# A hybrid encoder layer: the output projection's weight sums made in another stage, and its first weight splits set one step behind their loads

## The chip, the cores and the metric

The kernel runs on one core of a Trainium2 chip. The metric is the device time of one execution in microseconds (us). Times are compared by the median of several runs.

## What is computed

One layer works on 2048 tokens of width 1024, in float32 throughout. Cut to what matters here, the reference is:

```python
u = rms_norm(h, g_mix_pre)
z = u @ w_in                                   # 1024 -> 2816 columns
qa, ka, va, qh, fh, ih, gh = split(z)
ya = swa_with_sinks(qa, ka, va, sinks)         # 8 heads of 64, window of 128 tokens
yh = hgrn2(qh, fh, ih, gh, lb, onorm)          # gated linear recurrence, 4 heads of 128, chunks of 64
y = concatenate([ya, yh]) @ w_out              # 1024 -> 1024, the "out projection"
h = h + rms_norm(y, g_mix_post)
h = h + rms_norm(cross_attention(rms_norm(h, g_x_pre), rms_norm(mem, g_mem), ...), g_x_post)
u = rms_norm(h, g_ffn_pre)
h = h + rms_norm((silu(u @ w_gate) * (u @ w_up)) @ w_down, g_ffn_post)
```

## The kernel before

**Products.** Every large product is made of float32 operands split in two parts, a rounded high part (ScalarE or GpSimd copies it) and the rest (VectorE subtracts it); three products of parts stand for one. Blocks of two token tiles or two column tiles go through a seven-product scheme (Strassen's, in Winograd's form): a block has seven steps of 12 matmuls of 128x512 (`seven`), and needs sums and differences of the quarters of both operands. The streamed operand's sums are made block by block (`streamed`, L1106). The other operand, of which four plain quarters and four sums are used by all blocks of a product, is called resident here (`resident`, tiles `T`). For weights, its sums are made once ahead and kept in a DRAM tensor: `sums` and `combined` load the quarters, add or subtract them on VectorE (L1034) and store the four results, in two halves each. That is eight VectorE operations, 20 loads and eight stores for `w_out`, whose tensor is `out_s`. `combined` is a generator: for each of the eight results it issues the loads, returns three times, and at the fourth call adds and stores.

**Stages.** `in_first` makes the input projection for the first 1024 tokens, with the seven-product scheme, from 0 to about 260 us. Eleven pairs of column blocks (`ORDER`) pass through it; four pairs hold a forget gate and its query (`fh`, `qh`), and after each of these comes `decays` (scan, exponentials, logarithm) on ScalarE, VectorE and GpSimd. `mix` then interleaves, up to about 630 us, three generators by hand: the rest of the input projection (`in_proj`, three products per split pair, no sums), the sliding-window attention (`swa`) and the recurrence (`hgrn`, one pair of chunks per call). Then, up to about 770 us, the last recurrence pairs run beside `fold_cross`, which multiplies the cross-attention's weights together. The remaining products (out projection, scores, values, feed-forward) follow in `phases`, out of pools of their own, to the end.

**Where the sums of w_out are made.** In `mix`, beside the second half of the attention: four calls of the generator `side` per attention pair. They use the tiles `u` (two buffers) and `x` (three), which the decays of `in_proj` use too.

**Where the first resident halves are made.** `phases` begins with a prologue for the out projection: eight halves of four `T` tiles. Each call loads one half into a tile `z` (two buffers, which hold the projected columns of `in_proj` too) and splits it at once. The loop over the last recurrence pairs calls it eight times, from the second pair on. All these loads are issued on SP's queue.

**Order.** Each engine and queue works in order. That order is not the order of the code alone: `TileContext(nc, schedule_with_timeline_sim=True)` lets a planner take, for each engine, the instruction that is ready first on a simulated timeline, with the order of the code as priority. `queued` and `behind` add edges that keep an instruction behind another one; `combined` uses `behind`, so that each sum stands behind the VectorE work of the step at which it is made. An instruction that fills a tile can be placed only once a buffer of that tile is free.

Of the kernel before, what the change touches and what calls it, by code (L numbers as in the profile page):

```python
# [11 lines left out]
F32 = mybir.dt.float32  # L12
# [6 lines left out]
P = 128  # L19
T = 2048  # L20
D = 1024
# [27 lines left out]
class Layer:  # L49
# [144 lines left out]
    def mix(self):  # L194
        tc, I = self.tc, self.I
        kw = dict(reuse_waits="tile")
        with contextlib.ExitStack() as left:
            def pool(name, at, **k):
                return at.enter_context(tc.tile_pool(name=name, bufs=1, **k, **kw))

            self.mc = pool("mc", left)
            self.r_x = self.cst.tile([P, NT], F32, name="r_x")
            with (
                tc.tile_pool(name="t1", bufs=3, **kw) as self.ts,
                tc.tile_pool(name="t2", bufs=3, **kw) as self.tb,
                tc.tile_pool(name="s1", bufs=2, side="right", **kw) as self.st_pool,
                contextlib.ExitStack() as at,
            ):
                self.banks(at, "ps1", **MOST)
                self.raws = 3  # L210
                u = self.in_first()
            self.banks(left, "ps2", **FOUR)
            self.hg = pool("hg", left)
            self.wp = pool("wp", left)
            self.io = pool("io", left)
            with tc.tile_pool(name="sw", bufs=1, side="right", **kw) as self.sw:
                self.zero_tiles()
                swa = self.swa(range(NT), lambda n: "st" if n < NPB else "sth")
                hgrn = self.hgrn(range(NPB), "h")
                cols = self.in_proj(1, u)  # L220
                next(cols)
                for _ in range(NPB + 1):
                    next(swa)
                    next(hgrn)
                    next(cols)
                for _ in hgrn:
                    pass
                self.out_sums, side = self.sums("out_s", self.w_out, 4, lambda: self.io_tile("u"), lambda: self.io_tile("x"))
                side = side()
                next(side)  # L230
                pairs = self.hgrn(range(NPB, NT), "gt")
                for i, _ in enumerate(swa, NPB + 2):
                    next(cols)
                    if i == NT + 1 - 0:
                        next(pairs)
                    for _ in range(4):
                        next(side, None)
                for _ in cols:
                    pass
            phases = self.phases(self.jobs(), None, lambda: self.io_tile("z"))  # L240
            with tc.tile_pool(name="xp", bufs=1, side="right", **kw) as self.xp:
                fold = self.fold_cross()
                for _ in range(2):
                    next(fold)
                for i, _ in enumerate(pairs, 1):
                    for _ in range(2):
                        next(fold)
                    if 2 <= i < 10:
                        next(phases)
                for _ in fold:  # L250
                    pass
            left.close()
            with (
                tc.tile_pool(name="t3", bufs=3, **kw) as self.ts,
                tc.tile_pool(name="t4", bufs=3, **kw) as self.tb,
                tc.tile_pool(name="s3", bufs=2, side="right", **kw) as self.st_pool,
                contextlib.ExitStack() as at,
            ):
                self.banks(at, "ps3", **MOST)
                self.raws = 4  # L260
                for _ in phases:
                    pass
# [188 lines left out]
    def in_first(self):  # L451
# [13 lines left out]
        T, raw = {}, {}  # L465
# [51 lines left out]
        def fetch():  # L517
            for s in range(2):
                for q in range(2):
# [9 lines left out]
        blocks = [("s",) + self.in_block(*p, tokens[i], tokens[i + 1], beside[i + 1], get if i > 9 else (), i < 2,  # L529
                                         None if i else lambda: x_loads(0, (2, 3)))  # L530
                  for i, p in enumerate(self.ORDER)]
# [1 line left out]
        plain = [b[1:4] + ([],) for b in blocks[:2]]  # L533
        blocks[:2] = ([(k, stream, out, lambda: iter(()), keep) for k, (stream, out, _, keep) in zip("qu", plain)]
                      + [("v", lambda kind: iter([None]), out, after, keep) for _, out, after, keep in plain])
        phases = self.phases([(lambda i, j, a, n: raw[i, j][:, a:a + n, :], 4, blocks, None, {})], T)
        PE, ACT, DVE, POOL = (getattr(mybir.EngineType, e) for e in ("PE", "Activation", "DVE", "Pool"))
        next(phases)
        self.turns("h", 36)
# [45 lines left out]
        u = []  # L585
# [633 lines left out]
    def phases(self, jobs, first, prologue=None):  # L1219
# [17 lines left out]
        T, keep = {}, [{} for _ in jobs]  # L1237
# [24 lines left out]
        def split(g):  # L1262

            if pending and pending[0][0] <= g:
                _, k, f = pending.pop(0)
                f()
                left[k] -= 1
                return True
            return False
# [54 lines left out]
                made[0] += 1  # L1324

        if not first:
            for i in range(8):
                half(-1, prologue)
                split(len(steps))
                yield  # L1330
        stream(0)
        yield
# [458 lines left out]
```

## Time and profile before

| | us |
|---|---|
| three timed runs, median (lowest to highest) | 2554.95 (2553.55 to 2556.43) |
| profiled execution, its own time | 2550.01 |
| span of the profiled execution, first to last instruction | 2548.3 |
| TensorE busy in it | 2504.8 |
| VectorE busy in it | 1792.1 |
| ScalarE busy in it | 1261.6 |
| mean granted TensorE clock | 0.997 |

The span is what the trace covers; the time of the profiled execution is 1.7 us longer, and the median of the timed runs 4.9 us longer still. In the profile's rows PE is TensorE, PEld its weight loads, DVE VectorE, ACT ScalarE, POOL GpSimd and SP the queue that issues the transfers. L990 and the like are lines of the kernel. A row of a timeline gives start, length, engine, line, operation, the tile written and those read, shape, count, and in brackets the idle time of the engine before it and what ended that. A row of stretches gives the stretch, its length, the busy time of PE, PEld, DVE, ACT and POOL, each with its number of instructions, the granted clock, the DMA share and GB/s.

### The profile page before, as it was taken

To read this page: it belongs to the slowest core of one execution; us is meant where nothing else is said; L and a number is where in the kernel's file an instruction comes from. 1 tells how busy PE (TensorE), PEld (TensorE's weight loads), DVE (VectorE), ACT (ScalarE), POOL (GpSimd) and SP (SyncE) were. 2 spreads that over 40 slices of the span, in tenths; PEclk is the share of its full clock that TensorE was granted. 3 is DMA by queue.
4 is the path that set the end of the run, shared out by engine and by line. 5 is a ranking of instruction groups with operands and counts; after the bars stand their busy time and mean duration, and the time that the engine had idled before them with its cause. 6 is when DMAs were issued, how large, how long until landed. Compare 5 with 4: busy or idle time off the path is not lost.

```text
span 2548.3 us, 34324 instructions
## 1 busy us (share of the span) xinstructions
PE 2504.8 (98%) x12006; PEld 2092.8 (82%) x12006; DVE 1792.1 (70%) x2871; ACT 1261.6 (50%) x2635; POOL 364.6 (14%) x540
## 2 busy tenths in 40 slices
PE   9999999999999999999999999999999999999998
PEld 8878888877997778878878888888888888878886
DVE  8885488987556989988876555576566557574766
ACT  5553466655555566566753333353333335443543
POOL 4231234321311112102200000000000000000022
PEclk9999999999999999999999999999999999999999
DMA  6455655865887996867954522254465434564786
GB/s 201 146 165 178 192 154 170 230 204 146 259 292 275 316 335 189 274 206 226 333 200 146 177 91 87 74 203 148 160 210 195 144 117 159 180 188 106 228 177 151
DMA packets 387885, 486.33 MB, mean 191 GB/s; under 512 B 22272, under 2 KB 283392, under 8 KB 387712
## 3 DMA queue, kind: packets, MB, share of 16 engines
q1 hardware_dynamic: 381664, 462.12, 55.9%
q0 software_dynamic: 6048, 22.02, 5.0%
q8 instruction: 94, 1.54, 0.2%
q14 instruction: 79, 0.65, 0.1%
HBM read 317.34 MB, written 166.72 MB: 190 GB/s over the span
## 4 chain that ended last, share of the span: by engine, by line
PE 51%; DVE 2%; DMA 1%; issue 1%; ACT 1%; POOL 0%; SPq 0%; DVEq 0%; POOLq 0%; ACTq 0%
PE psm L1133 17%; PE psm L1131 17%; PE psm L1132 17%; DVE T L990 0%; DVE S L990 0%; ACT junk L1504 0%; PE pss L1390 0%; DMA out_dram<-row 0%; DMA row<-d_s 0%; DMA row<-in_w_down_dram 0%; DMA u_d<-row 0%; DMA sraw<-in_w_gate_dram 0%; DVE sum L1106 0%; ACT S L987 0%; ACT T L987 0%
## 5 line engine op out<-in xcount | busy, mean ns | idle before, releaser
L1131 PE MATMUL psm<-T,S 128*128 128x512 f32 x2680 | 1034.1, 390 | 13.3 <-ACT part L1146 7.2
L1132 PE MATMUL psm<-T,S 128*128 128x512 f32 x2680 | 1042.3, 390 | 4.0 <-DVE T L990 3.9
L1133 PE MATMUL psm<-T,S 128*128 128x512 f32 x2680 | 1029.4, 389 | 4.1 <-DVE S L990 4.1
L1131 PEld LDWEIGHTS psm<-T,S 128*128 128x128 f32 x2680 | 503.0, 188 | 125.9 <-ACT part L1146 11.9
L1132 PEld LDWEIGHTS psm<-T,S 128*128 128x128 f32 x2680 | 503.2, 188 | 110.5 <-DVE T L990 7.3
L1133 PEld LDWEIGHTS psm<-T,S 128*128 128x128 f32 x2680 | 503.1, 188 | 110.6 <-DVE S L990 6.3
L987 ACT ACTIVATE S<-sum 128x512 fp32r<-128x512 f32 (+1 forms) x370 | 224.0, 620 | 371.5 <-PE psm L1133 267.3
L990 DVE TENSOR_TENSOR S<-sraw,S 128x512 fp32r<-128x512 f32 (+1 forms) x315 | 211.5, 679 | 218.8 <-ACT S L987 215.8
L1146 ACT ACTIVATE part<-psm 128x512 f32<-128x512 f32 x285 | 168.6, 596 | 251.9 <-PE psm L1133 230.9
L990 DVE TENSOR_TENSOR S<-sum,S 128x512 fp32r<-128x512 f32 (+1 forms) x388 | 257.4, 673 | 42.1 <-ACT S L987 38.3
L987 ACT ACTIVATE S<-sraw 128x512 fp32r<-128x512 f32 (+1 forms) x300 | 184.7, 618 | 110.8 <-PE psm L1133 106.0
L1537 POOL DMA_DIRECT2D y_d<-row x16 | 14.1, 879 | 1077.9 <-DVE row L1721 1027.6
L990 DVE TENSOR_TENSOR T<-row,T 128x1024 fp32r<-128x1024 f32 (+1 forms) x112 | 131.0, 1183 | 30.2 <-ACT T L987 29.2
L157 PE MATMUL psg<-u,whi 128*128 128x512 f32 x320 | 128.3, 401 | 0.0
L158 PE MATMUL psg<-u,wlo 128*128 128x512 f32 x320 | 127.6, 399 | 0.0
L156 PE MATMUL psg<-u,whi 128*128 128x512 f32 x320 | 127.5, 399 | 0.0
L1504 ACT ACTIVATE junk<-row 128x512 f32<-128x512 f32 x160 | 99.6, 624 | 40.6 <-DVE row L1526 20.6
L987 ACT ACTIVATE T<-row 128x1024 fp32r<-128x1024 f32 (+1 forms) x112 | 113.3, 1031 | 7.5 <-DMA row<-d_s 4.3
L1672 DVE TENSOR_TENSOR row<-psm,part 128x512 f32<-128x512 f32 x66 | 43.7, 687 | 66.9 <-PE psm L1133 66.9
L1681 DVE TENSOR_TENSOR part<-psm,part 128x512 f32<-128x512 f32 x66 | 43.8, 687 | 60.1 <-PE psm L1133 59.8
L1721 DVE TENSOR_TENSOR row<-psm,part 128x512 f32<-128x512 f32 x72 | 49.1, 688 | 49.5 <-PE psm L1133 49.4
L814 ACT ACTIVATE S<-S,w_mn 128x256 f32<-128x256 f32 (+1 forms) x128 | 63.0, 496 | 29.6 <-DVE w_mn L810 29.2
(363 smaller groups left out, 3562.2 us busy)
## 6 DMA issues: line engine op xcount, KB each, us to landing
sraw<-in_w_gate_dram SPq DMA_DIRECT2D x44, 512.0 KB, 3.6
sraw<-in_w_up_dram SPq DMA_DIRECT2D x44, 512.0 KB, 3.7
hid_d<-row SPq DMA_DIRECT2D x44, 512.0 KB, 2.7
sraw<-hid_d SPq DMA_DIRECT2D x32, 512.0 KB, 4.2
sraw<-in_w_in_dram SPq DMA_DIRECT2D x44, 256.0 KB, 4.0
z_d<-pair SPq DMA_DIRECT2D x20, 512.0 KB, 3.4
raw<-in_w_in_dram SPq DMA_DIRECT2D x20, 512.0 KB, 4.8
z_d<-z SPq DMA_DIRECT2D x20, 512.0 KB, 4.0
```

What stands on the lines that cost most here:

```text
L156: nc.tensor.matmul(ps, ah, bh, start=(i == 0), stop=False)
L157: nc.tensor.matmul(ps, ah, bl, start=False, stop=False)
L158: nc.tensor.matmul(ps, al, bh, start=False, stop=(i == n - 1))
L814: nc.scalar.activation(s[:, r, o:], s[:, r, o:], AF.Exp, bias=mn[:, i:i + 1], scale=-1.0, accum_out=den[:, i:i + 1])
L987: self.nc.scalar.activation(hi, raw, AF.Copy)
L990: self.nc.vector.tensor_tensor(lo, raw, f32(hi), ALU.subtract)
L1131: nc.tensor.matmul(ps, s[:, 0, k, :], t[:, 0, k, :], start=st, stop=False, **kw)
L1132: nc.tensor.matmul(ps, s[:, 0, k, :], t[:, 1, k, :], start=False, stop=False, **kw)
L1133: nc.tensor.matmul(ps, s[:, 1, k, :], t[:, 0, k, :], start=False, stop=sp, **kw)
L1146: nc.scalar.activation(t, ps, AF.Copy)
L1504: self.nc.scalar.activation(junk, a, AF.Square, scale=float(D) ** -0.5, accum_out=to)
L1721: nc.vector.tensor_tensor(d, a, b, ALU.add)
```

## The change

The change has two parts.

The weight sums of `w_out` leave `mix` and are made in `in_first`. They get two tiles of their own (`wa` and `wb`, one buffer each, in a pool of the input projection). The generator is started at the fifth entry of the projection's block list, the first one that goes through the seven-product scheme, and is then advanced once per step. Its 33 calls thus take four blocks and five steps, among them the blocks with the decays.

In the prologue of `phases` the split of a half is done one call after its load, so there are nine calls instead of eight; the loop over the recurrence pairs begins to call at the first pair instead of the second. Each half's split so stays in the same pair as before, and each load is written one pair earlier. The input projection's own use of `phases` doesn't go through this prologue.

```diff
@@ mix @@
                 for _ in hgrn:
                     pass
-                self.out_sums, side = self.sums("out_s", self.w_out, 4, lambda: self.io_tile("u"), lambda: self.io_tile("x"))
-                side = side()
-                next(side)
                 pairs = self.hgrn(range(NPB, NT), "gt")
                 for i, _ in enumerate(swa, NPB + 2):
                     next(cols)
                     if i == NT + 1 - 0:
                         next(pairs)
-                    for _ in range(4):
-                        next(side, None)
...
                 for i, _ in enumerate(pairs, 1):
                     for _ in range(2):
                         next(fold)
-                    if 2 <= i < 10:
+                    if i < 10:
                         next(phases)
@@ in_first @@
+        def weight_tile(tag):
+            self._n += 1
+            return self.st_pool.tile([P, D], F32, tag=tag, name=f"{tag}_{self._n}", bufs=1)
+
+        self.out_sums, side = self.sums("out_s", self.w_out, 4, lambda: weight_tile("wa"), lambda: weight_tile("wb"))
-        phases = self.phases([(lambda i, j, a, n: raw[i, j][:, a:a + n, :], 4, blocks, None, {})], T)
+        phases = self.phases([(lambda i, j, a, n: raw[i, j][:, a:a + n, :], 4, blocks, None, {4: [side]})], T)
@@ phases @@
         if not first:
-            for i in range(8):
-                half(-1, prologue)
-                split(len(steps))
+            for i in range(9):
+                if i < 8:
+                    half(-1, prologue)
+                if i:
+                    split(len(steps))
                 yield
```

What the moved generator does at each call (not changed):

```python
def put(key, t, o, op):
    with self.behind():
        nc.vector.tensor_tensor(t, t, o, op)
    self.store(dst[self.CHAIN.index(key), :, a * 512:b * 512], t.rearrange("p k d -> p (k d)"))
```

## The prediction

> **What bounds the kernel now.** I read the engines' shares first, then busy time by stretches, then TensorE's waits, and last the timelines around the places that the change touches. The page's first part:
>
> ```profile
> PE 2504.8 (98%) x12006; PEld 2092.8 (82%) x12006; DVE 1792.1 (70%) x2871; ACT 1261.6 (50%) x2635; POOL 364.6 (14%) x540
> ```
>
> TensorE sets the time, and the change adds no matmul and takes none away. It can only move the 2548.3 - 2504.8 = 43.5 us in which TensorE idles. Its three places are the input projection (the sums arrive), the second half of the mixing stage (they leave) and the fold stage (the splits are moved). First the input projection, in stretches cut where a block's third partial-sum copy starts, so each is one block of seven steps:
>
> ```profile
> 75.00:100.00 25.00, 25.00 (x112) 20.70 (x111) 14.83 (x22) 8.17 (x15) 5.92 (x9) 1.00 0.64 190
> 91.40:111.20 19.80, 19.30 (x85) 15.68 (x84) 14.88 (x20) 10.91 (x16) 6.32 (x9) 1.00 0.42 122
> 111.20:131.50 20.30, 19.35 (x85) 15.70 (x85) 18.04 (x25) 12.82 (x20) 9.54 (x11) 1.00 0.51 156
> 131.50:152.00 20.50, 19.30 (x85) 15.66 (x85) 19.21 (x26) 12.93 (x20) 9.38 (x11) 1.00 0.50 154
> 152.00:172.30 20.30, 19.35 (x86) 15.69 (x85) 19.16 (x26) 12.82 (x20) 9.88 (x11) 1.00 0.59 181
> 172.30:191.40 19.10, 19.10 (x86) 15.80 (x85) 13.71 (x21) 6.93 (x13) 3.20 (x6) 1.00 0.47 167
> PE psm L1131 <- ACT part L1146: 3.6, 4, 1.2
> ```
>
> After the stretch come its length, then busy time of PE, PEld, DVE, ACT and POOL. An undisturbed block lasts 19.10 us, TensorE full. The blocks with decays last 20.3 to 20.5, and there VectorE is busy 18.04 to 19.21: it has 1.1 to 2.3 us to spare per block. The last line (waits of TensorE, 60 to 180 us) shows what TensorE loses: a wait for a ScalarE copy, four times. The chain behind one of them, from the timelines:
>
> ```profile
> 120.16 1.28 DVE L644 TENSOR_TENSOR pair<-psm,part 128x512 f32<-128x512 f32 x2
> 121.49 0.62 ACT L650 ACTIVATE pair<-pair 128x512 f32<-128x512 f32 x1
> 122.22 2.70 POOL L652 TENSOR_SCALAR pair<-pair,fb,fa 128x512 f32<-128x512 f32 x1 [1.28 <-ACT pair L650]
> 124.95 1.06 ACT L730 ACTIVATE pair<-pair 128x1024 f32<-128x1024 f32 x1 [1.54 <-POOL pair L652]
> 127.82 0.59 ACT L1146 ACTIVATE part<-psm 128x512 f32<-128x512 f32 x1
> 128.46 0.50 PE L1131 MATMUL psm<-T,S 128*128 128x512 f32 x1 [0.95 <-ACT part L1146]
> ```
>
> VectorE's addition (L644) frees the tanh on ScalarE, GpSimd scales, ScalarE takes the logarithm, and only then copies the partial sum that TensorE needs. Whatever holds VectorE before L644 holds TensorE at the end.
>
> **Part 1: the sums arrive.** The same work in the kernel before, and when the first block that carries them begins:
>
> ```profile
> L1034 DVE TENSOR_TENSOR u<-u,x x6: 1198/1214/1224, 448.1 to 521.9; 128x1024 f32<-128x1024 f32 x6
> L1034 DVE TENSOR_TENSOR x<-x,u x2: 1206/1216/1225, 494.4 to 523.6; 128x1024 f32<-128x1024 f32 x2
> 66.94 0.60 ACT L1146 ACTIVATE part<-psm 128x512 f32<-128x512 f32 x1 [0.22 <-ACT T L987]
> ```
>
> That is eight VectorE operations of 1.2 us, 9.7 us in all. The generator is advanced once per step of 19.1 / 7 = 2.73 us and computes at every fourth, queued behind that step's last VectorE operation. Step 1 of the carrying block ends at 66.7 us; so the operations come at about 75, 86, 97, 108, 119, 131, 143 and 155 us, the last three moved by the blocks' own 1.2 us of stalls. Those at 75 and 86 find VectorE busy only 14.83 of 25 us. The stretch from 91.4 gets two (97, 108): 14.88 + 2.4 = 17.3 of 19.8, they fit. From 111.2, one: 18.04 + 1.2 = 19.2 of 20.3, fits. From 131.5, two (131, 143): 19.21 + 2.4 = 21.6, which is 1.1 more than 20.5. From 152.0, one: 19.16 + 1.2 = 20.4, 0.1 too many. By throughput the cost is at least 1.2 us. But these two blocks run with 20.5 - 19.21 = 1.3 and 20.3 - 19.16 = 1.1 us of VectorE idle although it is what holds them; if that idle, spent waiting inside the chain, can't be filled, they cost 2.4 and 1.2, so 3.6. If from 108 on nothing is absorbed, five operations cost 6.0. I take 3.6, which the rows of the two full blocks carry; the range keeps 1.2 to 6.0. Queued behind each operation on VectorE are the block's lower-half splits and L644; who waits is the chain above.
>
> The transfers move too: 20 loads and 8 stores on SP's queue.
>
> ```profile
> 440.00 0.60 SPq L75 DMA_DIRECT2D u<-in_w_out_dram  x1
> 449.29 0.34 SPq L78 DMA_DIRECT2D out_s<-u  x1
> DMA to landing us min/median/max: 2.6/6.0/10.9
> 116.59 0.92 SPq L75 DMA_DIRECT2D sraw<-in_w_in_dram  x2
> 124.36 1.09 DVE L1106 TENSOR_TENSOR sum<-sraw,sraw 128x512 f32<-128x512 f32 x1
> sraw<-in_w_in_dram SPq DMA_DIRECT2D x44, 256.0 KB, 4.0
> ```
>
> Issuing costs 20 x 0.6 + 8 x 0.34 = 15 us of SP over some 90 us. With one buffer per tile, the reload waits for the store from it to land, and the queue waits with it: the third row is the landing of the tensor of sums, its stores and later reads together, 6.0 at the median. Behind stand the next block's weight loads: issued by 117.5, landed 4.0 later, used at 124.36, so 2.9 us are free. I price this at nothing; if that cover goes, 6.0 - 2.9 = 3.1 us at one block. DMA load (0.42 to 0.59 in these blocks) leaves room.
>
> **Part 2: the sums leave 440 to 526 us.** TensorE and VectorE there:
>
> ```profile
> 490.00:500.00 10.00, 9.90 (x48) 7.91 (x47) 9.94 (x26) 5.75 (x20) 2.60 (x5) 1.00 1.13 282
> 510.00:520.00 10.00, 9.56 (x48) 7.35 (x47) 9.04 (x28) 5.44 (x17) 1.31 (x2) 1.00 1.05 329
> 520.00:530.00 10.00, 9.27 (x51) 7.74 (x50) 5.52 (x7) 3.88 (x8) 6.33 (x6) 1.00 0.87 302
> 530.00:540.00 10.00, 9.27 (x46) 6.92 (x45) 9.73 (x31) 5.60 (x18) 1.55 (x5) 1.00 0.51 139
> 521.91 1.22 DVE L1034 TENSOR_TENSOR u<-u,x 128x1024 f32<-128x1024 f32 x1 [2.76 <-DMA out_s<-u]
> 523.78 0.39 PE L805 MATMUL psh<-kh,qs 128*128 128x256 f32 x1 [0.73 <-DVE ys L853]
> ```
>
> VectorE is full to 520, and one sum even stands 2.76 us for a transfer with the attention's work behind it; TensorE then loses 0.73. From 490 to 530 TensorE's listed idle is 0.10 + 0.44 + 0.73 = 1.3, in four late starts; a matmul is listed 0.39 long but repeats every 0.23 (19.1 / 84), so each late start hides some 0.16 more, 2.0 together. All of it should go: -2.0. Bounds: 0, if the attention's own VectorE work then ends last, and -3.2, if the three late starts from 530 to 540 (0.73 + 3 x 0.16 = 1.2) go too, which I doubt: VectorE was busy only 5.52 of the 10 us before, so the sums had left it no backlog.
>
> **Part 3: splits one pair behind their loads.**
>
> ```profile
> L987 ACT ACTIVATE T<-z x8: 1057/1060/1063, 622.4 to 662.6; 128x1024 fp32r<-128x1024 f32 x8
>   DMA z<-in_w_out_dram: 17.5, 8
> 616.97 1.26 SPq L75 DMA_DIRECT2D z<-in_w_out_dram  x2
> 622.39 1.06 ACT L987 ACTIVATE T<-z 128x1024 fp32r<-128x1024 f32 x1 [3.71 <-DMA z<-in_w_out_dram]
> 623.49 1.23 DVE L990 TENSOR_TENSOR T<-z,T 128x1024 fp32r<-128x1024 f32 x1 [3.46 <-ACT T L987]
> 623.84 0.60 PE L902 MATMUL pst<-ident,v 128*128 128x128 f32 x4
> 624.74 1.25 SPq L75 DMA_DIRECT2D z<-in_w_out_dram  x2
> 626.04 0.59 SPq L75 DMA_DIRECT2D v<-z_d  x1
> 630.78 1.04 PE L902 MATMUL pst<-ident,v 128*128 128x128 f32 x4 [2.59 <-DMA v<-z_d]
> 626.00:630.00 4.00, 2.19 (x18) 1.95 (x16) 2.26 (x3) 0.69 (x2) 0.00 (x0) 1.00 0.99 246
> 630.00:634.00 4.00, 3.11 (x12) 2.55 (x12) 2.72 (x4) 3.81 (x6) 0.00 (x0) 0.61 1.06 285
> ```
>
> ScalarE waits 17.5 us for these loads, but it has little to do here (0.69 busy of the 4 us from 626); TensorE's own loss is the 2.59 us for v, and after it the granted clock is 0.61 over 4 us, another 4 x 0.39 = 1.6. v was issued behind the second load, and that load waited for a z buffer: the first split ends at 623.49 + 1.23 = 624.72, the load goes at 624.74. There are two z buffers, and the other still holds the last projected column. The edit adds none. Issue order comes from a planner that takes what is ready, not from the order of the code; each split stays in the same pair, and the earlier load still has no buffer. So I expect the same queue: 0. Bounds: -4.2 (the stall and its clock) and, if another load is caught likewise, +2.6.
>
> **Sum.** 3.6 - 2.0 + 0 = +1.6 us. The profiled execution took 2550.01 us (span 2548.3), so 2551.6; the three timed runs have their median 4.94 above it, at 2554.95, so 2556.6 on that scale. 0.2% is 5.1 us, about what a measurement can tell from no change.
>
> **Rivals.**
> *Stalls that cost the clock (slower).* With nothing absorbed, the full blocks' stalls grow from 1.2 to 1.2 + 2.4 = 3.6 and 1.2 + 1.2 = 2.4 us. The 2.59 us stall above was followed by a half clock; the 1.2 us stalls are not (clock 1.00 in their rows). If two blocks cross a threshold between these, it is 6.0 + 2 x 1.6 - 2.0 = +7.2: 2562.2. It decides from a stall of some 2.6 us on. Against it: that the slack of 1.1 to 1.3 us absorbs some. [...]
> *The lag works (faster).* If the planner puts v ahead of the second load, stall and clock go, -4.2; with half the cost in part 1 (1.8) and -3.2 in part 2 this is -5.6: 2549.3. For: v needs only TensorE's previous transposes, over at 623.84 + 0.60 = 624.4, before the buffer was free. Against: the earlier load has no buffer, as said.
> *The sums find room and the lag does nothing (the edit doesn't do what it says).* 1.2 - 2.0 = -0.8: 2554.2. For: VectorE idles 1.1 to 2.3 us in each of these blocks; against: it idles there although TensorE waits for it.
>
> **How the numbers follow.** Forecast 0.34 (within 0.2%), third rival 0.10 (within), clock rival 0.31 (slower), working lag 0.25 (faster): 0.25, 0.44, 0.31. The forecast's own range is +1.6 with 1.2 to 6.0 and 0 to -3.2 around it: -2.0 to +6.0, 2553 to 2561. For 8 in 10 I reach to the greater part of both outer cases: -7.0 to +8.5, 2548.0 to 2563.5.
>
> **What would show it.** L1034 between 75 and 160 us on tiles wa and wb. Blocks around 131 to 172 us longer by 1 to 2.4 each. Granted clock 1.00 there, or the first rival is right. Waits at 490 to 525 us gone. In the fold stage, v still issued behind the second z load and its 2.59 us still there, or the second rival is right. Wrong altogether, if a stage after 780 us changes, which the edit doesn't touch.

## The result and the profile after

| | us |
|---|---|
| changed kernel, median of 6 runs | 2573.52 (2572.02 to 2573.94) |
| kernel before, 6 runs beside it | 2554.25 (2552.34 to 2556.43) |
| ratio, 95% interval | 1.0075 (1.0062 to 1.0088) |
| profiled execution, its span | 2572.2 (before 2548.3) |

The change costs 19 us, outside the range on record and beyond its dearest rival (2562.2). The two spans differ by 23.9; 4.2 of that is that the profiled execution of before lies below its median, and 0.4 that the other lies above. The page's first part of the changed kernel:

```profile
PE 2512.6 (98%) x12006; PEld 2098.6 (82%) x12006; DVE 1791.8 (70%) x2871; ACT 1260.7 (49%) x2635; POOL 365.4 (14%) x540
```

The counts of instructions are the same as before, and VectorE and ScalarE are busy for the same time. TensorE is "busy" 7.8 us longer with the same matmuls, which is the first sign of a slower clock (0.994 granted in the mean, against 0.997); its idle grows from 43.5 to 59.6. The stretches by stage, first before, then after (length, busy PE, PEld, DVE, ACT, POOL, clock, DMA share, GB/s). They are cut at 62 us and where TensorE starts the first matmul of the mixing stage, the first transpose of the fold stage, and the first seven-step block after it:

```profile
0.00:62.00 62.00, 58.69 (x350) 52.05 (x351) 50.88 (x66) 35.45 (x64) 28.49 (x46) 1.00 0.65 199
62.00:262.70 200.70, 196.60 (x862) 161.18 (x861) 147.03 (x202) 91.90 (x143) 55.81 (x71) 1.00 0.54 167
262.70:624.70 362.00, 357.85 (x1973) 304.81 (x1972) 285.80 (x700) 215.49 (x620) 114.20 (x181) 1.00 0.61 180
624.70:774.30 149.60, 143.81 (x1089) 136.05 (x1088) 79.51 (x113) 84.90 (x196) 30.86 (x41) 0.99 0.85 269
774.30:2548.30 1774.00, 1747.90 (x7737) 1438.74 (x7735) 1228.87 (x1793) 833.84 (x1615) 135.21 (x203) 1.00 0.60 189
```

```profile
0.00:62.00 62.00, 55.31 (x327) 48.51 (x328) 45.75 (x58) 34.37 (x61) 27.71 (x44) 0.97 0.72 200
62.00:281.00 219.00, 206.66 (x884) 168.35 (x884) 162.08 (x215) 93.32 (x145) 57.88 (x71) 0.98 0.67 199
281.00:632.90 351.90, 349.26 (x1950) 299.33 (x1949) 274.55 (x693) 213.57 (x618) 110.71 (x182) 1.00 0.51 154
632.90:795.40 162.50, 151.44 (x1114) 142.83 (x1113) 80.63 (x113) 85.74 (x197) 30.40 (x40) 0.98 0.80 252
795.40:2572.20 1776.80, 1749.94 (x7737) 1439.57 (x7735) 1228.76 (x1793) 833.65 (x1615) 138.72 (x203) 1.00 0.61 189
```

The input projection ends 18.3 us later (281.0 against 262.7). The mixing stage is 10.1 shorter and the fold stage 12.9 longer. Part of both is only a shifted border: 23 to 25 matmuls, some 5 us, change from one to the other. Together they are 2.8 longer. The rest is 2.8 longer too. 18.3 + 2.8 + 2.8 = 23.9. (The experiments below show how far one execution differs from another in these stages.)

**The input projection.** TensorE's waits from 62 to 281 us in the changed kernel (waiting for, us in total, times, longest):

```profile
PE psm L1131 <- ACT part L1146: 9.8, 5, 6.2
PE psm L1131 <- DVE pair L644: 2.5, 1, 2.5
```

Before, these were 4.1 us in five waits, none over 1.2. The longest one, followed back on the timelines of the changed kernel (start, length, engine, line, operation; in brackets the idle before and what ended it; L424 and L426 are L429 and L431 of before):

```profile
95.39 1.21 DVE L1034 TENSOR_TENSOR wa<-wa,wb 128x1024 f32<-128x1024 f32 x1
96.62 0.34 SPq L78 DMA_DIRECT2D out_s<-wa  x1
97.72 0.56 SPq L78 DMA_DIRECT2D z_d<-pair  x1
100.72 0.63 SPq L75 DMA_DIRECT2D pair<-in_x_dram  x1
107.67 1.06 ACT L424 ACTIVATE pair<-pair 128x1024 f32<-128x1024 f32 x1 [6.66 <-DMA pair<-in_x_dram]
109.76 1.63 DVE L426 SCALAR_TENSOR_TENSOR pair<-pair,n_r,g 128x1024 f32<-128x1024 f32 x1 [4.89 <-POOL n_r L104]
111.32 0.68 DVE L644 TENSOR_TENSOR pair<-psm,part 128x512 f32<-128x512 f32 x1
112.77 2.64 POOL L652 TENSOR_SCALAR pair<-pair,fb,fa 128x512 f32<-128x512 f32 x1 [2.45 <-ACT pair L650]
115.45 1.06 ACT L730 ACTIVATE pair<-pair 128x1024 f32<-128x1024 f32 x1 [1.49 <-POOL pair L652]
118.31 0.59 ACT L1146 ACTIVATE part<-psm 128x512 f32<-128x512 f32 x1
118.95 0.79 PE L1131 MATMUL psm<-T,S 128*128 128x512 f32 x1 [6.20 <-ACT part L1146]
```

And the two transfers that matter, in the kernel before:

```profile
89.55 0.42 SPq L78 DMA_DIRECT2D z_d<-pair  x1
91.96 0.60 SPq L75 DMA_DIRECT2D pair<-in_x_dram  x1
```

Read from the top: VectorE makes a sum, its store waits for it at the head of SP's queue, and behind that store stand the store of a projected column pair and a load of x. The x load goes at 100.72 instead of 91.96. Of these 8.8 us some 5.3 are older: TensorE had done 23 matmuls less by 62 us. The other 3.5 are the queue's. ScalarE takes the square of that x tile (L424) in its order, so it waits 6.66 us (1.65 before) and everything behind it waits too; VectorE waits 4.89 for the factor of the normalization, which GpSimd makes from that square. Only then come the addition L644, the scaling, the logarithm and the copy that TensorE needs. The chain from L644 on is the one that the prediction named. What it didn't name is what enters it from above.

**The clock.** The first row below is the stretch that follows this stall. The others lie around a stall of 1.72 us that both kernels have in the later stages, at 843.5 after and at 822.4 before (first after, then before):

```profile
118.08:124.91 6.83, 5.96 (x14) 4.70 (x15) 6.75 (x9) 2.26 (x5) 2.31 (x2) 0.50 0.66 205
841.71:845.12 3.41, 1.33 (x5) 0.76 (x5) 1.78 (x3) 3.29 (x8) 0.96 (x1) 1.00 1.10 383
845.12:848.53 3.41, 3.41 (x9) 2.65 (x9) 3.41 (x6) 0.45 (x1) 1.79 (x3) 0.50 1.08 342
```

```profile
818.60:822.01 3.41, 2.10 (x10) 1.41 (x8) 2.76 (x5) 1.38 (x5) 1.47 (x3) 1.00 1.04 392
822.01:825.42 3.41, 2.63 (x10) 1.90 (x11) 2.17 (x3) 2.47 (x6) 2.18 (x3) 1.00 1.12 375
```

Half clock comes in pieces of 3.41 us, each worth at most 1.7, half of its length: in the last row of the changed kernel a matmul of 128x512 starts every 0.43 us, and ahead of the stall every 0.23. Before the tail of the kernel, the changed one has seven of them (at 49.8, two from 118.1, 182.9, 650.6, 712.0, 845.1) and the one before two (279.3, 630.9): 5 x 1.7 = 8.5 at most of the 23.9 us.

**The fold stage** of the changed kernel, and then one row of before:

```profile
644.14 0.52 SPq L78 DMA_DIRECT2D z_d<-z  x1
644.71 0.43 SPq L75 DMA_DIRECT2D v<-z_d  x1
643.90 0.92 PE L886 MATMUL psg<-qq,k 128*128 128x192 f32 x4 [1.65 <-DVE z L713]
648.22 1.06 ACT L987 ACTIVATE T<-z 128x1024 fp32r<-128x1024 f32 x1 [3.98 <-DMA z<-in_w_out_dram]
649.82 0.49 PE L925 MATMUL pst<-vt,atz 128*128 128x128 f32 x2 [3.73 <-ACT vt L904]
```

```profile
628.75 2.29 SPq L78 DMA_DIRECT2D z_d<-z  x1
```

The last projected columns are finished so late that their store (z_d<-z) goes at 644.14, 11.2 us behind the stage's start at 632.9; before it was 4.1 (628.75 against 624.7). The next recurrence pair's loads stand behind it. And ScalarE still waits for the weight loads (3.98), now with the recurrence's copy `vt` behind it and TensorE behind that (3.73).

### The profile page after: what moved, and what is told of

It is laid out like the page before. It is cut to its first block, busy times and chain, and to the rows that moved or that the text cites. A ratio compares the mean times of both kernels' runs of the same rounds, so it can differ in the third digit from the quotient of the medians.

```text
span 2572.2 us, 34336 instructions
## 1 busy us (share of the span) xinstructions
PE 2512.6 (98%) x12006; PEld 2098.6 (82%) x12006; DVE 1791.8 (70%) x2871; ACT 1260.7 (49%) x2635; POOL 365.4 (14%) x540
## 4 chain that ended last, share of the span: by engine, by line
PE 51%; DVE 2%; DMA 1%; ACT 1%; issue 1%; POOL 0%; SPq 0%; DVEq 0%; POOLq 0%; ACTq 0%
PE psm L1133 17%; PE psm L1131 17%; PE psm L1132 17%; DVE S L990 0%; PE pss L1392 0%; ACT junk L1506 0%; DVE T L990 0%; DMA row<-in_w_down_dram 0%; DMA u_d<-row 0%; DMA sraw<-in_w_gate_dram 0%; ACT T L987 0%; DVE sum L1106 0%; DMA u_s<-row 0%; ACT S L987 0%; DVE row L1723 0%
## 5 line engine op out<-in xcount | busy, mean ns | idle before, releaser
L1131 PE MATMUL psm<-T,S 128*128 128x512 f32 x2680 | 1036.5, 391 | 22.3 <-ACT part L1146 13.9
L1131 PEld LDWEIGHTS psm<-T,S 128*128 128x128 f32 x2680 | 504.2, 188 | 135.9 <-ACT part L1146 19.0
L1133 PEld LDWEIGHTS psm<-T,S 128*128 128x128 f32 x2680 | 504.3, 188 | 111.1 <-DVE S L990 6.4
L987 ACT ACTIVATE S<-sraw 128x512 fp32r<-128x512 f32 (+1 forms) x300 | 184.8, 618 | 118.4 <-PE psm L1133 109.8
L1106 DVE TENSOR_TENSOR sum<-sraw,sraw 128x512 f32<-128x512 f32 (+1 forms) x97 | 65.7, 677 | 16.4 <-DMA sraw<-in_w_in_dram 7.3
```

Source lines behind the costliest of these rows:

```text
L987: self.nc.scalar.activation(hi, raw, AF.Copy)
L1106: nc.vector.tensor_tensor(t, a, b, op)
L1131: nc.tensor.matmul(ps, s[:, 0, k, :], t[:, 0, k, :], start=st, stop=False, **kw)
L1133: nc.tensor.matmul(ps, s[:, 1, k, :], t[:, 0, k, :], start=False, stop=sp, **kw)
```

## The experiments

All stages below are cut as above, from one profiled execution of each kernel; "mix + fold" is taken together because their border shifts. "Half" counts the pieces of half clock before the tail. The ratio is to the kernel before, run beside it on the same chip.

One execution against one leaves a spread. The input projection came out at 262.3 to 263.4 in the three kernels that don't touch it (before, lag alone, lag with three z buffers). Mix + fold came out at 510.5 to 516.7 in the five that leave these stages as they were (before, additions alone, transfers alone, sums in both places, x moved). The rest, which no kernel edits, came out at 1774.0 to 1780.2. So differences of some us in these last two columns can't be told from none.

| kernel | input projection | mix + fold | rest | half | ratio (95%) |
|---|---|---|---|---|---|
| before | 262.7 | 511.6 | 1774.0 | 2 | 1 |
| changed | 281.0 | 514.4 | 1776.8 | 7 | 1.0075 (1.0062 to 1.0088) |
| sums moved, no lag | 279.8 | 513.6 | 1774.5 | 6 | 1.0068 (1.0046 to 1.0091) |
| lag alone | 262.3 | 512.2 | 1775.3 | 1 | 0.9994 (0.9984 to 1.0005) |
| additions alone | 274.2 | 512.5 | 1777.3 | 4 | 1.0040 (1.0024 to 1.0057) |
| sums moved, on GpSimd's queue | 286.9 | 515.5 | 1777.5 | 11 | 1.0092 (1.0071 to 1.0113) |
| transfers alone | 275.8 | 516.7 | 1778.9 | 6 | 1.0061 (1.0044 to 1.0078) |
| sums in both places | 280.7 | 510.5 | 1777.5 | 5 | 1.0081 (1.0066 to 1.0096) |
| held loads | 274.5 | 516.2 | 1776.5 | 7 | 1.0051 (1.0034 to 1.0067) |
| late sums | 267.8 | 520.8 | 1777.9 | 6 | 1.0060 (1.0045 to 1.0075) |
| held loads, x on GpSimd's queue | 279.5 | 518.1 | 1774.9 | 7 | 1.0063 (1.0048 to 1.0078) |
| late sums, column ahead | 266.9 | 511.2 | 1779.0 | 4 | 1.0017 (1.0007 to 1.0026) |
| late sums, column ahead, every third step | 269.0 | 508.4 | 1776.3 | 2 | 1.0013 (1.0004 to 1.0022) |
| lag with three z buffers | 263.4 | 518.0 | 1776.2 | 3 | 1.0006 (0.9996 to 1.0015) |
| x moved (base) | 267.0 | 514.5 | 1777.3 | 5 | 1.0020 (1.0011 to 1.0030) |
| held loads, x moved | 274.9 | 511.9 | 1774.7 | 5 | 1.0035 (1.0021 to 1.0048) |
| held loads, x moved, column ahead | 277.7 | 504.3 | 1780.2 | 5 | 1.0020 (1.0010 to 1.0031) |

**Which part costs.** Part 1 alone (the prologue as before), and part 2 alone (the sums as before):

```diff
-            for i in range(9):
-                if i < 8:
-                    half(-1, prologue)
-                if i:
-                    split(len(steps))
+            for i in range(8):
+                half(-1, prologue)
+                split(len(steps))
```

> Only the first part of the change: the sums are made in the input projection; the prologue is the one of before. Theory Q (the moved transfers hold SP's queue, and with it the loads that ScalarE and VectorE wait for) and rival V (the moved additions hold VectorE) expect the same here: the input projection takes some 18 us more than before, as in the changed kernel, the mixing stage 2 to 4 less. If the fold stage's loss of some 7 us in the changed kernel comes from the second part, this kernel is 14 to 16 us slower than before; if that loss only follows from the moved sums, 19 to 22.

> Only the second part: splits one call behind their loads; the sums stay in the mixing stage. If the lag does nothing, because the planner already takes what is ready and the z tiles have two buffers, the time is that of before within 2 us. If the lag itself costs the fold stage, 4 to 7 us slower. If it works as meant, up to 4 us faster.

Part 1 alone ("sums moved, no lag" in the table) is 1.0068, part 2 alone 0.9994: the loss is the sums'. With the lag the v load still stands behind the second z load (624.12 behind 622.82), and TensorE waits for it 2.05 us (2.59 before):

```profile
628.50 0.63 PE L902 MATMUL pst<-ident,v 128*128 128x128 f32 x4 [2.05 <-DMA v<-z_d]
```

**Additions without transfers.** The kernel before, plus eight additions of two tiles that no transfer touches, at the steps of the moved sums:

```diff
+            for _ in range(8):
+                for _ in range(3):
+                    yield
+                with self.behind():
+                    nc.vector.tensor_tensor(wa, wa, wb, ALU.add)
+                yield
```

> The kernel before, with eight more VectorE additions of 128x1024 on two idle tiles at the steps of the input projection where the changed kernel makes the sums, and none of the 28 transfers there; their result is not used. Theory V: most of the 18 us in the input projection, so 12 to 18 us slower than before. Theory Q: only the VectorE work itself, 1.2 to 6.0 us as worked out in the prediction, no stall of TensorE over 3 us and clock 1.00 from 60 to 190 us.

The input projection is 11.5 us longer, and the total (1.0040, some 10 us) lies between the two expectations. One block of it:

```profile
127.82 1.21 DVE L546 TENSOR_TENSOR wa<-wa,wb 128x1024 f32<-128x1024 f32 x1
127.93 0.64 ACT L663 ACTIVATE pair<-pair 128x512 f32<-128x512 f32 x1 [0.81 <-DVE pair L657]
134.79 0.79 PE L1144 MATMUL psm<-T,S 128*128 128x512 f32 x1 [3.91 <-ACT part L1159]
```

TensorE's waits from 62 us to the stage's end come to 10.2 us, against 4.1: 6.1 more. Two pieces of half clock follow them, 3.4. By 62 us TensorE has done 340 matmuls instead of 350, another 2.3. That is 11.8, against 11.5 measured. But these 2.3 are not the additions': the stall that makes them stands at 16.89, and the first addition runs at 78.31.

```profile
16.89 0.39 PE L1145 MATMUL psm<-u,S 128*128 128x256 f32 x1 [2.95 <-DVE u L498]
78.31 1.22 DVE L546 TENSOR_TENSOR wa<-wa,wb 128x1024 f32<-128x1024 f32 x1
```

Between 12 and 17 us VectorE's operations stand in another order in this kernel than in the one before, where the wait at this place is 0.49. That leaves 11.5 - 2.3 = 9.2 for the additions. Eight operations of 1.2 us thus cost TensorE nearly their whole length, because the stalls take the clock with them.

**The transfers on another queue.**

```diff
-            self.load(d, self.I["w_out"][...])
+            (self.nc.gpsimd.dma_start if self.moved else self.load)(d, self.I["w_out"][...])
```

The stores of the sums are moved likewise.

> The first part alone, with the 28 transfers of the sums issued from GpSimd's queue instead of SP's. Theory Q: the stalls of the input projection at 36 to 53, 118 and 182 us go or shrink to those of the adds, so 1 to 6 us slower than before, at best equal. Rival V: as slow as the first part alone, 14 to 16 us. GpSimd's own issue time could add its own delay to the scaling that the decays wait for.

It is the slowest of all. GpSimd's order now holds these transfers among its own operations of the same chain (the factors of the normalization and the scaling): one store waits 6.86 us there for its sum and goes at 98.48. The x load, though still on SP's queue, goes at 103.35, 11.4 later than before, while the kernel is 6.0 behind (a partial-sum copy at 97.4 instead of 91.4). TensorE's waits in the stage are 16.2 us, the longest 7.6, and seven of the eleven pieces of half clock lie before 200 us. So this doesn't clear SP's queue of the charge; it shows that GpSimd's order has as little room.

**Transfers without additions.**

```diff
+                    self.store(scratch[...], (o if key == 4 else t).rearrange("p k d -> p (k d)"))
```

The generator's loads, not shown, are those of the sums; the line above stands in place of `put`.

> The kernel before plus the 28 transfers of the sums at the same steps of the input projection (20 weight loads and 8 stores through two one-buffer tiles, into a tensor that nothing reads), without the 8 additions; the sums stay in the mixing stage. Queue theory (the transfers on SP's queue hold back the x load that ScalarE and VectorE take in order): input projection 5 to 9 us longer than the 262.7 of before, the load pair<-in_x_dram issued about 8 us later than at 91.96, a TensorE stall behind L1146 near 115 to 119; total ratio 1.002 to 1.004. Rival (only the additions cost; the transfers delay a load that has slack): input projection within 2 us of before, ratio 1.000 to 1.001.

13.1 us in the input projection without one addition, more than either theory gave. With nothing to wait for but each other, the transfers bunch earlier, and the stalls stand at 76 and 82 us, not at 115, but their chains are of the same kind:

```profile
60.46 0.32 SPq L78 DMA_DIRECT2D scratch<-wa  x1
64.61 0.35 SPq L75 DMA_DIRECT2D pair<-in_x_dram  x1
69.72 1.06 ACT L429 ACTIVATE pair<-pair 128x1024 f32<-128x1024 f32 x1 [5.69 <-DMA pair<-in_x_dram]
76.16 0.50 PE L1154 MATMUL psm<-T,S 128*128 128x512 f32 x1 [2.79 <-ACT part L1169]
81.73 0.60 ACT L1169 ACTIVATE part<-psm 128x512 f32<-128x512 f32 x1 [5.10 <-DMA z_d<-zp]
82.38 0.79 PE L1154 MATMUL psm<-u,S 128*128 128x512 f32 x1 [2.75 <-ACT part L1169]
```

The x load goes 7.8 us later than before (56.83), twice what the kernel is behind as a whole; ScalarE waits for it, TensorE for ScalarE. Then a store of projected columns is late, its tile isn't free for the next partial sum, and ScalarE and TensorE wait again. TensorE's waits grow by 5.8 (9.9 against 4.1), two pieces of half clock add 3.4, and the 17 matmuls that are missing at 62 us (333 of 350; the first loads are issued at 18 us here too) another 3.9: 13.1. SP's queue alone does it. The two single costs don't add up: 9.2 + 13.1 = 22.3, while the sums moved cost 17.1 (3.4 by 62 us, 8.7 of waits, three pieces of half clock). Both end in the same chain, so that one delay can lie within the other; how much of it does wasn't measured.

**Sums in both places.** Is the longer fold stage carried over from the input projection, or does it come from taking the sums out of the mixing stage?

```diff
-        phases = self.phases([(..., blocks, None, {})], T)
+        _, side = self.sums("out_t", self.w_out, 4, lambda: weight_tile("wa"), lambda: weight_tile("wb"))
+        phases = self.phases([(..., blocks, None, {4: [side]})], T)
```

> The kernel before with the sums made in both places: in the input projection as in the changed kernel (into a second tensor that nothing reads) and still in the mixing stage. Theory (taking the sums out of the mixing stage lets the attention run ahead of the last projected columns and costs the fold stage 11 us): mixing stage about 361, fold about 151 us, input projection about 280 as with part 1 alone; total some 2 us below that of part 1 alone or equal to it, +14 to +18 us over before. Rival (the fold loss is carried over from the input projection, by what the queues still hold): fold 160 us or more and mixing stage 361, +26 us.

Mixing stage 359.8, fold 150.7, together 510.5, with the input projection as long as in the changed kernel. (The total of the timed runs, 21.9 over before, came out above what I gave; its interval and that of part 1 alone overlap.) So the fold stage's loss comes with the removal. With the sums gone (part 1 alone) the mixing stage is 352.2 and the fold stage 161.4, and 24 matmuls of the last projected columns stand behind the first transpose; in the kernel before and in this one none do. What the removal does to both stages together is less clear: 513.6 against 510.5 is 3.1 more, but that lies within the spread of 510.5 to 516.7. The six kernels without the sums there, with the order of the columns as it was and without the stall of the late kernel below, come out at 511.9 to 518.1. So the gain of 2.0 doesn't show, and a loss isn't shown either.

**The first loads held back.**

```diff
+        def held(*a):
+            with self.queued(self.traced(mybir.EngineType.SP)):
+                self.w_out(*a)
```

> Part 1 alone, with each weight load of the sums queued on SP behind the transfer that stands ahead of it in the code, so that the first ones can't be issued at 18 to 25 us ahead of the first weight loads of the projection. Theory: the stalls of 0.9 and 2.1 us at 36 and 48 us and the half clock after them go; input projection 3 to 5 us shorter than the 279.8 of part 1 alone, total about 2568; the stalls at 116 and 181 stay. Rival (the early loads don't matter, the start's stalls are those of the weight loads themselves): no change from part 1 alone, about 2572.

In the changed kernel SP issues the first four of these weight loads between 17.92 and 24.95, since their tiles are free, and the projection's own next weight loads, which before went from 18.26 to 28.12, only among and behind them. Held back, the first 62 us are as before (TensorE busy 58.87; 56.02 with part 1 alone) and the input projection is 5.3 shorter, 3.4 of it by 62 us (350 matmuls done; 335 with part 1 alone). That is what the theory said, slightly over its range; only the half clock near 50 us wasn't there in part 1 alone, but in the changed kernel. This kernel isn't late yet at 91.6, where it makes the copy that stood at 91.4 before, and still its x load goes at 96.48 instead of 91.96: these 4.5 us are the queue's. The next stall grew:

```profile
104.09 1.06 ACT L424 ACTIVATE pair<-pair 128x1024 f32<-128x1024 f32 x1 [7.39 <-DMA pair<-in_x_dram]
115.37 0.80 PE L1135 MATMUL psm<-T,S 128*128 128x512 f32 x1 [7.52 <-ACT part L1150]
```

**Late sums.** The kernel with the held loads, its generator started at the tenth entry:

```diff
-{4: [side]}
+{9: [side]}
```

> The previous kernel with the sums begun at the tenth group of columns instead of the fifth, in the blocks without decays, where VectorE is busy about 14 of 19 us. Theory (the loss is the additions in blocks that VectorE bounds, plus the x load held on SP): input projection within 3 us of before's 262.7, mixing stage 352, fold 161: total +2 to +6 us over before. Rival (an addition or transfer costs wherever it stands in this stage): input projection again 275 or more, total +15 us.

In light blocks the input projection is 5.1 us longer than before instead of 11.8: better than the rival, worse than the theory's 3. But the total didn't follow (16.0 us over before), for the transfers now reach the recurrence's first loads, which go 9.7 us later (vr<-z_d at 281.94, 272.26 before) although the stage is only 5.1 late, and three pieces of half clock come with the stall:

```profile
285.29 0.47 PE L790 MATMUL pss<-ident,vr 128*128 128x128 f32 x1 [4.68 <-DMA vr<-z_d]
```

**The x load on another queue.** Is it SP that holds the x load?

```diff
-                self.load(t[:, 0, :], self.I["x"][...])
+                nc.gpsimd.dma_start(t[:, 0, :], self.I["x"][...])
```

> The kernel with the held loads (part 1 alone, first sum loads held back), and the x tiles that the projection normalizes (pair<-in_x_dram, one per block) loaded through GpSimd's queue instead of SP's. Theory (the 7.7 us stall at 115.4 comes down the chain x load, square on ScalarE 7.39 late, normalization on VectorE, addition, logarithm, part copy): the square's wait falls below 2 us, the stall at 115 to 1 to 2 us, its 6.8 us half clock goes; input projection about 265 to 268 us instead of 274.5, total about 2560. Rival (the additions on VectorE hold the block anyway): the stall stays at 4 us or more, or comes again one block later, input projection 272 or more.

```profile
96.36 0.62 POOL L993 TENSOR_SCALAR S<-sum 128x512 fp32r<-128x512 f32 x1 [5.10 <-issue]
96.93 0.60 POOL L666 DMA_DIRECT2D pair<-in_x_dram  x1
```

The load didn't come earlier (96.93; 96.48 on SP): in GpSimd's order it stands behind L993. The input projection is 279.5, with stalls of 3.7 us at 113 and 4.7 at 140, the signs that the rival named. But since x wasn't early, the run says nothing on what happens when it is; as a cure it failed.

**The order of the mixing stage.** The late kernel, with one column taken ahead of the loop (in which the call becomes `next(cols, None)`):

```diff
+                next(cols)
                 pairs = self.hgrn(range(NPB, NT), "gt")
```

> The kernel with the late sums, and in the mixing stage one projected column more taken ahead of the second loop, so that the columns stand one step earlier in the code. Theory (without the sums the attention is placed ahead of the last columns, whose stores the next recurrence pair's loads wait for): the last z columns come ahead of the memory's transposes as before, fold stage 150 to 153 us instead of 160.4, mixing stage about as long as in the late kernel; total 2558 to 2560. Rival (the planner takes what is ready whatever the code's order): fold 160, no change.

The total came as the theory said, 2559.14. The measure that I named did not: the fold stage as cut is 162.6, since the border moved again (41 matmuls more lie behind it than in the late kernel). Together the two stages fall from 520.8 to 511.2. Up to 5.1 of that are three pieces of half clock less, one near 285, where the stall for vr (4.2) stays, and two in the fold stage. The planner does respond to the order of the code.

Then the same kernel with its generator returning two times instead of three before each sum:

> The previous kernel with the sums made at every third step instead of every fourth, so that their transfers end some 20 us earlier, before the recurrence's first loads. Theory (the 4.8 us stall for vr<-z_d at 285 us and the 10.2 us of half clock after it come from SP's queue, which is late by 10 us there): that stall goes, mixing stage 352 to 355 us instead of 360; total 2550 to 2555, level with before or just below. Rival (those loads wait for the last columns of the projection, whatever the queue holds): stall unchanged, 2558 to 2560 as in the previous kernel.

The wait for vr falls to 0.2: SP's queue had been the cause of that stall. Mix + fold is 508.4, 3.2 below before and 2.1 below the lowest of the kernels that leave it as it was. With an input projection of 269.0 the total is still 1.0013 of before, hardly less than the previous kernel's 1.0017; I had expected it level or below.

**Three z buffers for the lag.** The tile `z` gets `bufs=3`:

> Part 2 alone (the splits one pair behind their loads) with three z buffers instead of two. Theory of the prediction (the lag does nothing because the second load waits for a buffer that the first split frees): now the second load is issued before v, or v before it without delay; the 2.6 us stall at 630 to 631 and its half clock go, ScalarE's waits for z fall below 9 us of 17.5; total ratio 0.998 to 0.999. Rival (the loads and splits are placed by the planner where they are ready, a buffer more changes the order only): ratio 0.9995 to 1.001.

With a third buffer the wait for v is gone from TensorE's list, as the theory said. But a wait for k (1.7) takes its place, that for ScalarE's `atz` (1.9; 2.1 with the lag alone) stays, ScalarE's waits for z fall only to 15.1, and the total is as before (1.0006). So the buffer explains the one wait for v, and not why the lag brings nothing. The total is the rival's.

**x out of the decay blocks.** The x tiles are normalized beside light blocks:

```diff
-        beside = [(), (0,), (1, 2), (3,), (4,), (5,), (6,), (7,), (), (), (), ()]
+        beside = [(), (0, 1), (2, 3), (), (), (), (), (4, 5), (6, 7), (), (), ()]
```

> The kernel before with the last x tiles (four of seven groups) normalized beside light blocks instead of beside the blocks with decays, and the first two groups one block earlier; the sums stay in the mixing stage. It is the base for the next two. If x normalization in the decay blocks is what delays the chain to the partial-sum copy, the stalls of 1.1 to 1.4 us at 128, 149 and 169 us shrink below 0.5 and the input projection is 2 to 4 us shorter than 262.7: ratio 0.998 to 0.999. If it is the decays' own work on VectorE, they stay: 0.9995 to 1.001, or slower where the crowded blocks now stall.

And the held loads on this base:

> The kernel with the held loads (part 1 alone, first sum loads held back), x tiles moved out of the decay blocks as in the previous kernel. Theory (the x load that stands late on SP, and the square and normalization that wait for it ahead of the chain, make the stall): the 7.7 us stall at 115 and its 6.8 us half clock go, no stall over 2 us between 100 and 180 us, input projection 264 to 268 instead of 274.5; total 2557 to 2560. Rival (the additions' VectorE time in blocks that VectorE fills): stalls of 2 us or more in two or more of these blocks, input projection 270 or more, total 2564 or more.

The base alone is slower (1.0020): the stalls at 128 and 149 stay, and one of 3.2 at 171 comes in. On this base the 7.5 us stall near 115 is gone (0.5 at 109.8), as the theory said. Yet the stage is as long as with the held loads (274.9), as the rival said, for two others stand in it:

```profile
138.66 0.65 PE L1137 MATMUL psm<-u,S 128*128 128x512 f32 x1 [2.37 <-DVE S L994]
177.17 0.80 PE L1135 MATMUL psm<-u,S 128*128 128x512 f32 x1 [3.17 <-ACT S L991]
```

So that one stall came down the x chain, and the stage's cost is not that chain alone: over their own bases the held sums cost 11.8 us with x in the decay blocks and 7.9 without.

> The previous kernel with one projected column more taken ahead of the mixing stage's second loop, as in the kernel with the late sums. Theory (removing the sums is worth 2 to 3 us once the last columns' stores come in time): mixing and fold stage together 508 to 511 us, against 511.6 before and 516.2 with the held loads; 4 to 6 us below the previous kernel. Rival (the order is worth nothing here): 514 or more, no change.

Mix + fold falls to 504.3, 7.3 below before, further than expected. The total fell by 2.6, less than expected, since the input projection (277.7) and the rest (1780.2) came out longer. No kernel has the column ahead with the sums left in the mixing stage, so how much of this gain is the removal's and how much the order's alone stays open. No version with the sums moved beats the kernel before; the nearest is the late one with every third step.

## Why the prediction was wrong

**The step that failed first: the transfers priced at nothing.** "Behind stand the next block's weight loads ... 2.9 us are free. I price this at nothing." For those loads the slack was exceeded once (VectorE waits 2.06 us for one at 159.8 in the changed kernel). But the queue also carries the x loads and the stores of projected columns, and ScalarE and VectorE take both in their own order. Measured alone: 13.1 us instead of 0. The first loads, which nothing kept from being issued at 18 us, are a part of that: holding the loads back took 5.3 off the 17.1 of part 1 alone. The prediction asked when the generator's steps come, not when its loads could be placed.

**The additions, mis-sized.** 3.6 taken, 1.2 to 6.0 bounded, 9.2 measured (11.5 with the 2.3 that were lost before the first of them). The chain from L644 was right; in the changed kernel the additions ran at 81.2 to 178.1, not 75 to 155. With the additions alone its stalls are 6.1 more than before, as with nothing absorbed, and the half clock behind them 3.4: for this term the first rival, 6.0 + 2 x 1.6 = 9.2, had the mechanism and the size. The close agreement is in part luck, for its premise that a stall must reach some 2.6 us was wrong: the second piece of half clock follows a stall of 1.82 us, up to 157.5, while one of 2.3 us, up to 180.8, is followed by none.

**The removal, taken at -2.0 and not seen.** The waits at 490 to 525 went as said (from 440 to 540 TensorE keeps one wait of 0.7, at 519), and VectorE had room. But the prediction looked only at the stretch where the sums stood. Without them the planner puts attention ahead of the last columns: the mixing stage is some 8 us shorter, the fold stage 11 longer. Net that is +3.1 in one pair of executions, which is within their spread. With a column taken ahead the two stages come out at 511.2, 508.4 and 504.3, the last two lower than in any kernel that leaves them as they were; that this is the removal's gain, and not that of the order alone, isn't shown.

**The lag at 0: right** (0.9994, 0.9984 to 1.0005), and the rival that it works fell. The reason, a missing buffer, held for the wait for v alone: with the buffer that wait goes, and the lag gains nothing either.

**"Wrong altogether, if a stage after 780 us changes."** It did, by 2.8 us, though nothing in it was edited: up to 1.7 of that is the half clock behind a stall of 1.72 us that both kernels have. But over all these kernels that stage lasts 1774.0 to 1780.2, and with part 1 alone, the same half clock in it, 1774.5. So the sign was too sharp: a change of this size there says nothing against the mechanism.

**The sum.** +1.6 forecast, 19.3 measured by the medians. In the profiled executions, 23.9 apart: 17.1 in the input projection with part 1 alone, 1.2 more in the changed kernel, whose input projection is the same, 2.8 in mixing and fold, 2.8 behind; the last three are no more than the spread. What stays open: how the 17.1 divide between SP's queue (13.1 alone) and VectorE (9.2 alone), and why the x move left the stage at 275 us with other stalls in place of the first.

## What to carry to other kernels

Ask of a moved transfer what else stands behind it in its queue, and who takes that in order: here a store that waited for its addition held back an x load by some 3.5 us, and through ScalarE's order a copy that had nothing to do with either. A generator that is started later in the code can still have its first loads placed early, if their buffers are free; hold them back, which was worth 5.3 us here. Work taken out of a stage changes what a planner puts in its place, so read the border to the next stage too before booking a gain.

## What the runs showed of the hardware

The half clock doesn't begin at a stall but at fixed borders. In the changed kernel it begins at 49.81, 118.08, 182.93, 650.56, 712.00 and 845.12; these lie 20, 19, 137, 18 and 39 times 3.413 us apart (795.31 us from the first to the last, by 233). In the kernel before it begins at 279.28 and 630.86, 103 times as far apart; the border at 822.01 lies 159 times behind 279.28. What decided in these traces is how much TensorE idled between two such borders. The stall of 1.72 us in front of L1131, first after, then before:

```profile
843.52 0.50 PE L1131 MATMUL psm<-T,S 128*128 128x512 f32 x1 [1.72 <-ACT S L987]
```

```profile
822.43 0.50 PE L1131 MATMUL psm<-T,S 128*128 128x512 f32 x1 [1.72 <-ACT S L987]
```

At 843.52 it falls between two borders, together with a smaller one of 0.36 us (busy 1.33 of 3.41), and a half clock follows; at 822.43 the same two stalls lie on both sides of a border (2.10 and 2.63 busy), and none follows. In the traces of these two kernels, from 20 us to the end, TensorE's listed idle was over 0.56 of such a stretch at full clock eight times, and half clock followed each time. Closest to that share are two stretches of the changed kernel: 46.40 to 49.81 (busy 1.51 of 3.41) is followed by half clock, 111.25 to 114.67 (1.51 of 3.42) is not. Over all seventeen kernels it was over 0.56 in 50 stretches, and half clock followed each time; between 0.44 and 0.56 it followed 10 of 47 times, and below that only five times, all between 279 and 303 us: in the kernel before it is the one at 279.28, behind 2.33 busy of 3.41, with 12 of 14 matmuls 128x128 instead of 128x512. So here the same stall cost up to 1.7 us more or nothing by where it fell, and an edit that only shifts the later stages can change their time. The half clock at 845.12 followed a stretch in which the longest gap was 1.72 us and all idle time 2.08.
